# Gate and up of two SwiGLU layers from seven block products in place of eight

## The chip, the cores and the metric

The kernel runs on one core of a Trainium2 chip. Five engines work beside each other there: TensorE (PE in the profile) for matrix products, VectorE (DVE), ScalarE (ACT), GpSimd (POOL) and SyncE (SP), which here issues the loads; 16 transfer engines move the data. What counts is the device time of one execution in microseconds (us), the median over runs.

## What is computed

A trunk of two layers over 512 tokens of width 1024, float32. Each layer has a token mixer (differential attention in layer 0, a gated short convolution in layer 1) and a SwiGLU of hidden width 2816, each followed by a scaled residual and a layer norm. The change touches the SwiGLU:

```
def swiglu(x, w_gate, w_up, w_down):
    h = silu(x @ w_gate) * (x @ w_up)          # x: 512 x 1024, h: 512 x 2816
    return h @ w_down
...
    h = layer_norm(ALPHA * h + mixer(h), ln1_g[i], ln1_b[i])
    h = layer_norm(ALPHA * h + swiglu(h, ...), ln2_g[i], ln2_b[i])
```

## The kernel before

**A product.** TensorE multiplies float32r arrays. `split` (L52) turns a float32 array into two of them: the high part is a cast on ACT (L54), the low part a subtraction on DVE (L55). `mm3` (L70) then multiplies high by high, high by low and low by high, three products per pair of tiles, into one bank of PSUM, of which there are eight.

**Weights.** `weights` (L62) loads 512 KB as 128 x 1024 float32 into one of three `raw` buffers through SP's queue, and splits it into `whi` and `wlo`, six buffers of each. They serve all stages in turn, so that loads and splits run ahead of TensorE until the buffers are full.

**SwiGLU** (`swiglu`, L468). The hidden width is 22 tiles of 128 (`ft`). For one of them `load` fetches two weight tiles, gate and up in each; `part` issues 8 input tiles x 2 x 3 = 48 products with 512 columns, one column per token. `finish` takes silu of gate on ACT (L495), multiplies by up on DVE (L496) and splits the result into `hT`, which the down-projection reads. The first two tiles (`lead`) are done in two halves of 256 tokens, since the tokens of the second half aren't there yet: the normalization of the last two token tiles of the stage before runs meanwhile, and their transposes (`turns`) stand among the lead's products.

**Down-projection** (`project_norm`, L142). It goes over weight tiles of two feature tiles each and over four token tiles, adds the residual, and normalizes (`norm_tile`, L107), with two small operations on POOL for the inverse root. Its `turn` (L127) transposes a normalized token tile on TensorE and splits it into the next stage's input. The same function ends the attention and the convolution.

**Order.** A scheduler places each engine's instructions; each engine goes through its own row in that order, and waits for semaphores of the others. The order at a place can therefore be read from the built program, and its times from the trace.

## Time and profile before

| | us |
|---|---|
| device time, median of 3 runs | 1167.36 |
| lowest and highest of them | 1167.21, 1167.90 |
| span of the profiled execution | 1166.5 |
| TensorE busy in it | 1152.7 |
| DVE, ACT, POOL busy in it | 553.3, 373.3, 62.7 |

The profile is that of one execution. It gives its span, from the first instruction to the last; the device time of that same execution isn't listed apart. The span is 0.9 us below the median. In the rows, L72 is line 72 of the kernel before, a tile's name stands without its buffer number, and a product's tile name says what it serves: `gu` gate and up, `o_wo` and `o_dn` the projections back, `tp_` a transpose. The duration of a product in a row is modelled and overlaps the next one's; the distance from start to start is what counts. For an operation of another engine, the brackets behind it tell how long the engine was idle before it and what ended that. In layer 0 the SwiGLU begins at 252.0 us and its down-projection at 494.4 us; in layer 1 it begins at 795.4 us.

### The profile page before, as it was taken

How to read it: one execution, taken by the hardware profiler on the slowest of the kernel's cores; microseconds unless marked ns; L12 is line 12 of the kernel's file. 1: busy time of each engine (PE TensorE's matmuls, PEld its weight loads, DVE VectorE, ACT ScalarE, POOL GpSimd, SP SyncE). 2: the span in 40 equal slices, each digit the busy share in tenths (PEclk: the TensorE clock that was granted, in tenths of full speed). 3: DMA queues.
4: the chain of work that ended last, by engine and by line, in shares of the span. 5: the costliest groups of instructions: out<-in, count | busy, mean ns of one | idle time of the engine just before them, and what ended most of it. 6: DMA issues, size and time to landing. Idle time of an engine off the chain costs nothing.

```text
span 1166.5 us, 14313 instructions
## 1 busy us (share of the span) xinstructions
PE 1152.7 (99%) x5850; PEld 966.4 (83%) x5850; DVE 553.3 (47%) x861; ACT 373.3 (32%) x634; POOL 62.7 (5%) x83
## 2 busy tenths in 40 slices
PE   9999999999999999999999999999999999999997
PEld 7877787789888888888889888889888888888886
DVE  7777877684333333322355544457433333322316
ACT  5554645423223323311212423313322332321110
POOL 1111112020000000000010000011000000000002
PEclk9999999999999999999999999999999999999999
DMA  8421222134233233233313433323323323333302
GB/s 294 166 73 37 75 70 75 55 95 128 85 108 102 82 106 104 81 105 108 91 55 111 143 95 104 91 72 123 115 87 109 98 84 108 102 98 90 104 23 73
DMA packets 33490, 114.45 MB, mean 98 GB/s; under 512 B 3952, under 2 KB 4848, under 8 KB 33424
## 3 DMA queue, kind: packets, MB, share of 16 engines
q1 hardware_dynamic: 33424, 113.54, 30.8%
q8 instruction: 46, 0.75, 0.3%
q14 instruction: 20, 0.16, 0.0%
HBM read 111.42 MB, written 2.10 MB: 97 GB/s over the span
## 4 chain that ended last, share of the span: by engine, by line
PE 88%; DVE 6%; ACT 3%; POOL 1%; issue 1%; DMA 0%; SPq 0%; POOLq 0%; DVEq 0%; ACTq 0%
PE gu L74 14%; PE gu L72 14%; PE gu L73 14%; PE o_dn L73 7%; PE o_dn L74 7%; PE o_dn L72 7%; PE in L72 4%; PE in L73 4%; PE in L74 4%; ACT p L363 1%; PE o_wco L72 1%; PE o_wco L73 1%; PE o_wco L74 1%; DVE nm L360 1%; PE o_wo L72 1%; PE o_wo L74 1%
## 5 line engine op out<-in xcount | busy, mean ns | idle before, releaser
L72 PE MATMUL gu<-x_hi,whi_gu 128*128 128x512 f32 (+1 forms) x768 | 285.5, 372 | 0.0
L73 PE MATMUL gu<-x_lo,whi_gu 128*128 128x512 f32 (+1 forms) x768 | 285.2, 371 | 0.0
L74 PE MATMUL gu<-x_hi,wlo_gu 128*128 128x512 f32 (+1 forms) x768 | 285.2, 371 | 0.0
L55 DVE TENSOR_TENSOR wlo_gu<-raw_gu,whi_gu 128x1024 fp32r<-128x1024 f32 x88 | 107.7, 1223 | 244.2 <-ACT whi_gu L54 244.2
L73 PEld LDWEIGHTS gu<-x_lo,whi_gu 128*128 128x128 f32 x768 | 144.7, 188 | 25.1
L74 PEld LDWEIGHTS gu<-x_hi,wlo_gu 128*128 128x128 f32 x768 | 144.6, 188 | 25.1
L72 PEld LDWEIGHTS gu<-x_hi,whi_gu 128*128 128x128 f32 x768 | 144.7, 188 | 24.7
L54 ACT CAST whi_gu<-raw_gu 128x1024 fp32r<-128x1024 f32 x88 | 92.7, 1053 | 151.6 <-PE gu L73 130.2
L72 PE MATMUL o_dn<-whi_dn,hT_hi 128*128 128x512 f32 (+1 forms) x352 | 134.9, 383 | 0.0
L73 PE MATMUL o_dn<-wlo_dn,hT_hi 128*128 128x512 f32 (+1 forms) x352 | 134.8, 383 | 0.0
L74 PE MATMUL o_dn<-whi_dn,hT_lo 128*128 128x512 f32 (+1 forms) x352 | 134.6, 382 | 0.0
L55 DVE TENSOR_TENSOR wlo_dn<-raw_dn,whi_dn 128x1024 fp32r<-128x1024 f32 x44 | 53.9, 1224 | 161.9 <-ACT whi_dn L54 161.9
L54 ACT CAST whi_dn<-raw_dn 128x1024 fp32r<-128x1024 f32 x44 | 46.4, 1054 | 161.3 <-PE o_dn L74 117.8
L72 PE MATMUL in<-x_hi,whi_in 128*128 128x512 f32 (+1 forms) x240 | 83.3, 347 | 0.0
L73 PE MATMUL in<-x_lo,whi_in 128*128 128x512 f32 (+1 forms) x240 | 83.2, 347 | 0.0
L74 PE MATMUL in<-x_hi,wlo_in 128*128 128x512 f32 (+1 forms) x240 | 83.2, 347 | 0.0
L495 ACT ACTIVATE sg<-gu 128x512 f32<-128x512 f32 x44 | 26.3, 597 | 170.4 <-PE gu L74 170.4
L72 PEld LDWEIGHTS o_dn<-whi_dn,hT_hi 128*128 128x128 f32 x352 | 66.2, 188 | 13.1
L73 PEld LDWEIGHTS o_dn<-wlo_dn,hT_hi 128*128 128x128 f32 x352 | 66.2, 188 | 13.0
L74 PEld LDWEIGHTS o_dn<-whi_dn,hT_lo 128*128 128x128 f32 x352 | 66.1, 188 | 12.8
L72 PEld LDWEIGHTS in<-x_hi,whi_in 128*128 128x128 f32 x240 | 45.4, 189 | 5.7
L74 PEld LDWEIGHTS in<-x_hi,wlo_in 128*128 128x128 f32 x240 | 45.4, 189 | 5.7
(164 smaller groups left out, 1587.3 us busy)
## 6 DMA issues: line engine op xcount, KB each, us to landing
raw_gu<-in_wgu SPq DMA_DIRECT2D x88, 512.0 KB, 3.6
raw_dn<-in_wdn SPq DMA_DIRECT2D x44, 512.0 KB, 3.6
raw_in<-in_win SPq DMA_DIRECT2D x24, 512.0 KB, 3.5
raw_qk<-in_wqk SPq DMA_DIRECT2D x14, 512.0 KB, 3.6
raw_v<-in_wv SPq DMA_DIRECT2D x8, 512.0 KB, 4.1
raw_wo<-in_wo SPq DMA_DIRECT2D x8, 512.0 KB, 3.6
raw_wco<-in_wco SPq DMA_DIRECT2D x8, 512.0 KB, 3.7
res<-in_xT SPq DMA_DIRECT2D x8, 256.0 KB, 5.6
```

The lines of the kernel that those rows point to most:

```text
L54: nc.scalar.copy(hi, src)
L55: nc.vector.tensor_tensor(lo, src, hi.bitcast(F32), op=ALU.subtract)
L72: nc.tensor.matmul(out, lh, rh, start=first, stop=False)
L73: nc.tensor.matmul(out, lh, rl, start=False, stop=False)
L74: nc.tensor.matmul(out, ll, rh, start=False, stop=last)
L360: nc.vector.tensor_reduce(nm, ps[c][:, :n], axis=AX.X, op=ALU.max, negate=True)
L363: nc.scalar.activation(pc[:, :n], ps[c][:, :n], AF.Exp, bias=nm, accum_out=sm)
L495: nc.scalar.activation(sg, ps[0], AF.Silu)
```

## The change

Gate and up of two hidden tiles form a matrix of 1024 x 512, cut into four blocks: 11 and 21 are gate's upper and lower half of the input features, 12 and 22 are up's. The input is cut likewise: x11 and x12 are the two halves of the features for tokens 0 to 255, x21 and x22 those for tokens 256 to 511. Of the eight products of blocks, Strassen's form (in Winograd's variant) needs seven:

- 11 with x11 and 21 with x12 (their sum is gate of the first tokens, bank `x`)
- t2 with s2, t3 with s3, t4 with x22 (bank `y`), and t1 with s1, 22 with s4 (bank `z`)

where t1 = 12 - 11, t2 = 22 - t1, t3 = 22 - 12, t4 = 21 - t2 for the weights and s1 = x21 + x22, s2 = s1 - x11, s3 = x11 - x21, s4 = x12 - s2 for the input. A layer has 11 such units (`UNITS`). Each product is 24 matrix products with 256 columns (2 hidden tiles x 4 feature tiles x 3). The gate and up of both token halves come out of sums of the three banks, with seven operations on DVE a unit (`u2`, `w5`, `c21`, `h`), a copy `e` of the first product and two silus on ACT. Before the change that was one silu, one cast and two DVE operations per hidden tile.

The four sums of weights are computed on DVE and split as before (`combined`). The blocks 11, 21 and 22 are split in another way (`plain`): ACT writes the high part into `whi`, and minus the raw block, rounded to float32r and so minus the high part, into `wlo`; then a transfer issued by POOL adds the raw block to `wlo`, which leaves the low part. There are 33 of these transfers a layer, 512 KB each, from SBUF to SBUF.

The first three units (`LEAD`) begin with their products of 11 and 21 alone, which need only the first tokens. The two turns that are left over stand behind the first and the second of them; `turn_forms` now also computes the sums s1 to s4 and splits all seven forms of the input. Then these units' other five products follow, for which blocks 11 and 21 are loaded a second time: six loads more a layer, 100 in place of 88 in both. Raw blocks 11 and 22 use the three `raw` buffers, 12 and 21 two new ones (`raw2`).

The hidden `h` stays float32 (11 tiles of 128 x 1024 a layer) until the beginning of the down-projection, where ACT and DVE split it.

The core of the diff:

```diff
+HALF = S // 2
+UNITS = KF // 2
+LEAD = 3
...
+    def turn_forms(tt, r, x, name):
+        ts = slice((tt % 2) * P, (tt % 2 + 1) * P)
+        tps = []
+        for hf in range(2):
+            tp = bank(f"tp_{name}_{tt}_{hf}")
+            for j in range(4):
+                c = hf * 512 + j * P
+                nc.tensor.transpose(tp[:, j * P : (j + 1) * P], r[:, c : c + P], ident)
+            tps.append(tp.rearrange("p (k q) -> p k q", k=4))
+        def form(key, src):
+            hi, lo = x[key]
+            split(hi[:, :, ts], lo[:, :, ts], src)
+        a, b, c, d = (x["raw_" + key][:, :, ts] for key in ("x11", "x12", "x21", "s3"))
+        if tt < 2:
+            form("x11", tps[0])
+            nc.scalar.copy(a, tps[0])
+            form("x12", tps[1])
+            nc.scalar.copy(b, tps[1])
+            return
+        nc.scalar.copy(c, tps[0])
+        nc.vector.tensor_tensor(d, a, tps[0], op=ALU.subtract)
+        nc.vector.tensor_tensor(c, c, tps[1], op=ALU.add)
+        form("s1", c)
+        form("x22", tps[1])
+        nc.vector.tensor_tensor(a, c, a, op=ALU.subtract)
+        form("s2", a)
+        form("s3", d)
+        nc.vector.tensor_tensor(b, b, a, op=ALU.subtract)
+        form("s4", b)
...
-    def swiglu(i, xT, turns, xT_next, out):
+    def swiglu(i, x, turns, open_next, out):
...
-            def load(ft):
-                return [
-                    weights(t["wgu"][i, ft][:, 4 * g : 4 * g + 4, :], 4, 256, f"gu{i}_{ft}_{g}")
-                    for g in range(2)
-                ]
-            def part(ps, wgs, ts, after=()):
-                for n in range(2 * KD):
-                    k, j = (n % 8, n // 8) if ts.stop - ts.start == S else (n // 2, n % 2)
-                    wg, cs = wgs[k // 4], slice(j * P, (j + 1) * P)
-                    mm3(ps[j][:, ts], (wg[0][:, k % 4, cs], wg[1][:, k % 4, cs]),
-                        (xT[0][:, k, ts], xT[1][:, k, ts]), k == 0, k == KD - 1)
-                    for at, f in after:
-                        if at == n:
-                            f()
-            def finish(ft, ps):
-                sg = fwork.tile([P, S], F32, tag="sg", name=f"sg{i}_{ft}")
-                nc.scalar.activation(sg, ps[0], AF.Silu)
-                nc.vector.tensor_tensor(sg, sg, ps[1], op=ALU.mult)
-                split(hT[0][:, ft, :], hT[1][:, ft, :], sg)
-            lead = 2
-            wgs, pss = [], []
-            for ft in range(lead):
-                wgs.append(load(ft))
-                pss.append([bank(f"gu{i}_{ft}_{j}") for j in range(2)])
-            part(pss[0], wgs[0], slice(0, 256), [(8, turns[0])])
-            part(pss[1], wgs[1], slice(0, 256), [(5, turns[1])])
-            for ft in range(lead):
-                part(pss[ft], wgs[ft], slice(256, 512))
-                finish(ft, pss[ft])
-            for ft in range(lead, KF):
-                wg = load(ft)
-                ps = [bank(f"gu{i}_{ft}_{j}") for j in range(2)]
-                part(ps, wg, slice(0, S))
-                finish(ft, ps)
...
+            def blocks(u, keys):
+                out = {}
+                for key in keys:
+                    a, b = int(key[0]) - 1, int(key[1]) - 1
+                    tag, pool, n = ("raw", wpool, 3) if a == b else ("raw2", wk, 2)
+                    raw = pool.tile([P, 4, 256], F32, tag=tag, name=f"raw_gu{i}_{u}_{key}", bufs=n)
+                    nc.sync.dma_start(raw, t["wgu"][i, u, a, b])
+                    out[key] = raw
+                return out
+            def pair(name):
+                hi = wpool.tile([P, 4, 256], F32R, tag="whi", name=f"whi_{name}")
+                lo = wpool.tile([P, 4, 256], F32R, tag="wlo", name=f"wlo_{name}")
+                return hi, lo
+            def plain(raw, name):
+                hi, lo = pair(name)
+                nc.scalar.copy(hi, raw)
+                nc.scalar.activation(lo, raw, AF.Copy, scale=-1.0)
+                nc.gpsimd.dma_start(lo, raw, accum_op=ALU.add)
+                return hi, lo
+            def combined(raw, name):
+                hi, lo = pair(name)
+                split(hi, lo, raw)
+                return hi, lo
+            def tsum(a, b, op, name):
+                r = wk.tile([P, 4, 256], F32, tag="t", name=name, bufs=3)
+                nc.vector.tensor_tensor(r, a, b, op=op)
+                return r
+            def product(ps, w, key, first):
+                xh, xl = x[key]
+                for f in range(2):
+                    o = ps[:, f * HALF : (f + 1) * HALF]
+                    fs = slice(f * P, (f + 1) * P)
+                    for k in range(4):
+                        wh, wl = w[0][:, k, fs], w[1][:, k, fs]
+                        for n, (a, b) in enumerate(((wh, xh), (wh, xl), (wl, xh))):
+                            nc.tensor.matmul(o, a, b[:, k, :], start=first and f + k + n == 0,
+                                             stop=k == 3 and n == 2, skip_group_check=True)
...
+            def start(u, raw):
+                s = {"x": bank(f"x{i}_{u}")}
+                product(s["x"], plain(raw["11"], f"gu{i}_{u}_11"), "x11", True)
+                if u < LEAD:
+                    both = slot(slots["xa"], f"h{UNITS - 5 - u}", (2, 512), F32, f"lead{i}_{u}")
+                    s["e"], s["g"] = both[:, 0, :], both[:, 1, :]
+                else:
+                    s["e"], s["g"] = temp("e", u, 2), temp("g", u)
+                nc.scalar.copy(s["e"], s["x"])
+                return s
+            def second(u, s, raw):
+                product(s["x"], plain(raw["21"], f"gu{i}_{u}_21"), "x12", False)
+                nc.scalar.activation(s["g"], s["x"], AF.Silu)
+            def rest(u, s, raw, whole):
+                nm = f"gu{i}_{u}_"
+                v = nc.vector.tensor_tensor
+                t1 = tsum(raw["12"], raw["11"], ALU.subtract, nm + "t1")
+                t2 = tsum(raw["22"], t1, ALU.subtract, nm + "t2")
+                y = bank(f"y{i}_{u}")
+                product(y, combined(t2, nm + "t2"), "s2", True)
+                u2 = temp("u2", u)
+                v(u2, s["e"], y, op=ALU.add)
+                z = bank(f"z{i}_{u}")
+                product(z, combined(t1, nm + "t1"), "s1", True)
+                w5 = temp("w5", u)
+                v(w5, s["e"], z, op=ALU.add)
+                if whole:
+                    second(u, s, raw)
+                t3 = tsum(raw["22"], raw["12"], ALU.subtract, nm + "t3")
+                product(y, combined(t3, nm + "t3"), "s3", False)
+                v(w5, w5, y, op=ALU.add)
+                t4 = tsum(raw["21"], t2, ALU.subtract, nm + "t4")
+                product(z, plain(raw["22"], nm + "22"), "s4", False)
+                h = hidden(u)
+                hid[u] = h
+                v(u2, u2, z, op=ALU.add)
+                v(h[:, :, :HALF], s["g"].rearrange("p (f q) -> p f q", f=2),
+                  u2.rearrange("p (f q) -> p f q", f=2), op=ALU.mult)
+                product(y, combined(t4, nm + "t4"), "x22", False)
+                c21 = temp("c21", u)
+                v(c21, s["e"], y, op=ALU.add)
+                nc.scalar.activation(c21, c21, AF.Silu)
+                v(h[:, :, HALF:], c21.rearrange("p (f q) -> p f q", f=2),
+                  w5.rearrange("p (f q) -> p f q", f=2), op=ALU.mult)
+            state = {}
+            for u in range(LEAD):
+                state[u] = start(u, blocks(u, ("11",)))
+                if u < 2:
+                    turns[u]()
+            for u in range(LEAD):
+                second(u, state[u], blocks(u, ("21",)))
+            for u in range(UNITS):
+                if u < LEAD:
+                    rest(u, state[u], blocks(u, ("11", "12", "22", "21")), False)
+                else:
+                    raw = blocks(u, ("11", "12", "22", "21"))
+                    rest(u, start(u, raw), raw, True)
...
+            hT = []
+            for u in range(UNITS):
+                if u == 0:
+                    hi = wpool.tile([P, 2, S], F32R, tag="whi", name=f"hid{i}_{u}_hi")
+                    lo = wpool.tile([P, 2, S], F32R, tag="wlo", name=f"hid{i}_{u}_lo")
+                elif u < 8:
+                    hi, lo = (slot(slots["f"], f"f{2 * u - 2 + j}", (2, S), F32R, f"hid{i}_{u}_{j}") for j in range(2))
+                else:
+                    hi, lo = (slot(dx, f"d{2 * u + j}", (2, S), F32R, f"hid{i}_{u}_{j}") for j in range(2))
+                split(hi, lo, hid[u])
+                hT.append((hi, lo))
...
-    gu = np.stack([a["ffn_w_gate"].reshape(2, KD, P, KF, P), a["ffn_w_up"].reshape(2, KD, P, KF, P)], axis=4)
+    gu = np.stack([a[f"ffn_w_{n}"].reshape(2, 2, 4, P, UNITS, 256) for n in ("gate", "up")], axis=2)
```

**Where the order of work changes.** First ACT's row in the lead of layer 0, behind the last high part of the first blocks. Names: `lead0_0` is the copy of bank x of unit 0, `gu0_1_21` block 21 of unit 1, `x1_s3` a form of the input; L564 and L565 are the two ACT operations of `plain`, L57 a cast of `split`. Before:

```order
L54 CAST whi_gu0_2_0_3135<-raw_gu0_2_0_3133 128x1024
L54 CAST x1_hi_2353<-tp_wo_2_0_2930 128x4x128
L54 CAST x1_hi_2353<-tp_wo_2_1_2937 128x4x128
L54 CAST whi_gu0_2_1_3141<-raw_gu0_2_1_3139 128x1024
L54 CAST x1_hi_2353<-tp_wo_3_0_2983 128x4x128
L54 CAST x1_hi_2353<-tp_wo_3_1_2990 128x4x128
L54 CAST whi_gu0_3_0_3202<-raw_gu0_3_0_3200 128x1024
L495 ACT_TABLE_LOAD
L495 ACTIVATE sg0_0_3075<-gu0_0_0_2887 128x512
```

After:

```order
L608 COPY lead0_0_2933<-x0_0_2903 128x512
L189 COPY x1_raw_x21_2680<-tp_wo_2_0_2935 128x4x128
L564 CAST whi_gu0_0_21_3055<-raw_gu0_0_21_3053 128x1024
L57 CAST x1_s3_hi_2674<-x1_raw_s3_2681 128x4x128
L565 ACTIVATE wlo_gu0_0_21_3056<-raw_gu0_0_21_3053 128x1024
L57 CAST x1_s1_hi_2668<-x1_raw_x21_2680 128x4x128
L57 CAST x1_x22_hi_2670<-tp_wo_2_1_2940 128x4x128
L57 CAST x1_s2_hi_2672<-x1_raw_x11_2678 128x4x128
L57 CAST x1_s4_hi_2676<-x1_raw_x12_2679 128x4x128
L608 COPY lead0_1_2992<-x0_1_2962 128x512
L189 COPY x1_raw_x21_2680<-tp_wo_3_0_2994 128x4x128
L564 CAST whi_gu0_1_21_3087<-raw_gu0_1_21_3085 128x1024
```

Between the two operations on block 21 of unit 0 and those of unit 1 there are now the copies of the banks, which wait for TensorE, and the turns' casts; the second operation on block 21 of unit 1 (`L565 ACTIVATE wlo_gu0_1_21`) comes six rows further down.

Second, SP's row of loads at the same place; `raw_gu0_0_21` is block 21 of unit 0. Before:

```order
L64 DMA raw_gu0_2_0_3133<-in_wgu 128x1024
L64 DMA raw_gu0_2_1_3139<-in_wgu 128x1024
L64 DMA raw_gu0_3_0_3200<-in_wgu 128x1024
L64 DMA raw_gu0_3_1_3206<-in_wgu 128x1024
L102 DMA g_f0_4473<-in_ln2_g 128x1024
L103 DMA b_f0_4474<-in_ln2_b 128x1024
L64 DMA raw_gu0_4_0_3267<-in_wgu 128x1024
L64 DMA raw_gu0_4_1_3273<-in_wgu 128x1024
```

After:

```order
L552 DMA raw_gu0_0_21_3053<-in_wgu 128x1024
L552 DMA raw_gu0_1_21_3085<-in_wgu 128x1024
L114 DMA g_f0_5589<-in_ln2_g 128x1024
L115 DMA b_f0_5590<-in_ln2_b 128x1024
L552 DMA raw_gu0_2_21_3117<-in_wgu 128x1024
L552 DMA raw_gu0_0_12_3151<-in_wgu 128x1024
L552 DMA raw_gu0_0_21_3155<-in_wgu 128x1024
```

A load waits for its buffer. With two buffers for blocks 12 and 21, the load of 21 of unit 2 waits for the adding transfer of unit 0's block 21, the load of 12 of unit 0 for that of unit 1's, and the second load of 21 of unit 0 for that of unit 2's. All rows behind them on SP wait as well.

Third, DVE's row between two units in the middle of layer 0, where `gu0_9_t3` is a sum of weights and `wlo_gu0_9_t2` a low part. Before:

```order
L55 TENSOR_TENSOR wlo_gu0_10_0_3672<-raw_gu0_10_0_3669,whi_gu0_10_0_3671 128x1024
L496 TENSOR_TENSOR sg0_7_3530<-sg0_7_3530,gu0_7_1_3481 128x512
L55 TENSOR_TENSOR wlo_gu0_10_1_3678<-raw_gu0_10_1_3675,whi_gu0_10_1_3677 128x1024
L55 TENSOR_TENSOR hT_lo0_2874<-sg0_7_3530,hT_hi0_2873 128x512
L55 TENSOR_TENSOR wlo_gu0_11_0_3739<-raw_gu0_11_0_3736,whi_gu0_11_0_3738 128x1024
L496 TENSOR_TENSOR sg0_8_3597<-sg0_8_3597,gu0_8_1_3548 128x512
```

After:

```order
L58 TENSOR_TENSOR wlo_gu0_8_t4_5035<-gu0_8_t4_5000,whi_gu0_8_t4_5034 128x1024
L576 TENSOR_TENSOR gu0_9_t3_5203<-raw_gu0_9_22_5070,raw_gu0_9_12_5068 128x1024
L623 TENSOR_TENSOR u20_8_4906<-e0_8_4870,y0_8_4877 128x512
L627 TENSOR_TENSOR w50_8_4937<-e0_8_4870,z0_8_4908 128x512
L58 TENSOR_TENSOR wlo_gu0_9_t2_5113<-gu0_9_t2_5109,whi_gu0_9_t2_5112 128x1024
L58 TENSOR_TENSOR wlo_gu0_9_t1_5144<-gu0_9_t1_5107,whi_gu0_9_t1_5143 128x1024
L576 TENSOR_TENSOR gu0_9_t4_5234<-raw_gu0_9_21_5072,gu0_9_t2_5109 128x1024
L632 TENSOR_TENSOR w50_8_4937<-w50_8_4937,y0_8_4877 128x512
L576 TENSOR_TENSOR gu0_10_t1_5341<-raw_gu0_10_12_5302,raw_gu0_10_11_5300 128x1024
L637 TENSOR_TENSOR u20_8_4906<-u20_8_4906,z0_8_4908 128x512
L638 TENSOR_TENSOR h0_8_5031<-g0_8_4871,u20_8_4906 128x2x256
L58 TENSOR_TENSOR wlo_gu0_9_t3_5206<-gu0_9_t3_5203,whi_gu0_9_t3_5205 128x1024
```

For each hidden tile there were two low parts of weights, one product with up and one low part of the hidden. For each unit of two tiles there are now four sums, four low parts and seven operations on the banks; the weights are a unit ahead of the banks that they stand among.

## Rows read from the trace of the kernel before

**Rows 1.** The page: busy us, share, count by engine; granted clock in 40 slices.

```profile
PE 1152.7 (99%) x5850; PEld 966.4 (83%) x5850; DVE 553.3 (47%) x861; ACT 373.3 (32%) x634; POOL 62.7 (5%) x83
...
PEclk9999999999999999999999999999999999999999
```

**Rows 2.** Stretches: sum, then busy us of PE, PEld, DVE, ACT, POOL; PEclk, DMA.

```profile
252.00:276.00 24.00, 24.00 (x203) 23.99 (x202) 15.28 (x21) 8.51 (x11) 1.70 (x2) 1.00 0.48 155
276.00:494.00 218.00, 218.00 (x967) 180.64 (x966) 75.46 (x81) 64.96 (x81) 0.00 (x0) 1.00 0.31 99
```

**Rows 3.** Groups by shape: count, busy us, mean ns, idle us before.

```profile
L72 PE MATMUL gu<-x_hi,whi_gu 128*128 128x512 f32 x640 | 249.0, 389 | 0.0
...
L72 PE MATMUL gu<-x_hi,whi_gu 128*128 128x256 f32 x128 | 36.5, 285 | 0.0
...
L72 PEld LDWEIGHTS gu<-x_hi,whi_gu 128*128 128x128 f32 x768 | 144.7, 188 | 24.7
```

**Rows 4.** TensorE in time order, wide products: start us, duration us, instruction.

```profile
420.26 0.39 PE L72 MATMUL gu<-x_hi,whi_gu 128*128 128x512 f32 x1
...
435.90 0.39 PE L72 MATMUL gu<-x_hi,whi_gu 128*128 128x512 f32 x1
```

**Rows 5.** The same, narrow products of layer 0's lead.

```profile
252.00 0.28 PE L72 MATMUL gu<-x_hi,whi_gu 128*128 128x256 f32 x1
...
262.00 0.28 PE L72 MATMUL gu<-x_hi,whi_gu 128*128 128x256 f32 x1
...
271.71 0.28 PE L72 MATMUL gu<-x_hi,whi_gu 128*128 128x256 f32 x1
```

**Rows 6.** Tile o_dn (down-projections): ns min/median/max, first and last start.

```profile
L72 PE MATMUL o_dn<-whi_dn,hT_hi x352: 277/389/476, 494.4 to 1155.4; 128*128 128x512 f32 x172, 128*128 128x256 f32 x4
```

**Rows 7.** Groups of ACT and DVE, columns as in rows 3.

```profile
L54 ACT CAST whi_gu<-raw_gu 128x1024 fp32r<-128x1024 f32 x88 | 92.7, 1053 | 151.6 <-PE gu L73 130.2 <-PE o_wco L74 9.3 <-PE o_wo L74 7.5
...
L54 ACT CAST hT_hi<-sg 128x512 fp32r<-128x512 f32 x44 | 27.0, 613 | 0.0
...
L55 DVE TENSOR_TENSOR wlo_gu<-raw_gu,whi_gu 128x1024 fp32r<-128x1024 f32 x88 | 107.7, 1223 | 244.2 <-ACT whi_gu L54 244.2
...
L496 DVE TENSOR_TENSOR sg<-sg,gu 128x512 f32<-128x512 f32 x44 | 30.2, 687 | 30.1 <-PE gu L74 25.4 <-ACT sg L495 4.7
...
L55 DVE TENSOR_TENSOR wlo_wo<-raw_wo,whi_wo 128x1024 fp32r<-128x1024 f32 x8 | 11.2, 1402 | 3.3 <-ACT whi_wo L54 3.2
```

**Rows 8.** Transfers: packets, MB, engine share; issues: KB each, us to landing.

```profile
q1 hardware_dynamic: 33424, 113.54, 30.8%
...
raw_gu<-in_wgu SPq DMA_DIRECT2D x88, 512.0 KB, 3.6
...
res<-in_x SPq DMA_DIRECT2D x1, 2048.0 KB, 9.9
```

**Rows 9.** A group of POOL, columns as in rows 3.

```profile
L90 POOL TENSOR_TENSOR rstd_wo<-ve_wo,mhalf 128x1 f32<-128x1 f32 x4 | 3.7, 929 | 0.3
```

**Rows 10.** ACT in time order, layer 0's lead; brackets: idle us, releaser.

```profile
255.87 1.08 ACT L54 CAST x_hi<-tp_wo 128x512 fp32r<-128x512 f32 x2 [3.97 <-PE tp_wo L132]
...
261.41 1.08 ACT L54 CAST x_hi<-tp_wo 128x512 fp32r<-128x512 f32 x2 [3.44 <-PE tp_wo L132]
...
270.88 1.28 ACT L495 ACT_TABLE_LOAD   x1 [1.64 <-PE gu L74]
```

**Rows 11.** The same of ACT and POOL, end of the attention.

```profile
221.30 1.05 ACT L54 CAST whi_gu<-raw_gu 128x1024 fp32r<-128x1024 f32 x1 [0.81 <-PE o_wo L74]
...
222.95 0.70 POOL L405 TENSOR_SCALAR ms<-ms 128x2 f32<-128x2 f32 x1 [5.95 <-ACT on L403]
```

**Rows 12.** TensorE in time order at the start of the kernel.

```profile
7.38 0.63 PE L72 MATMUL k<-x_hi,whi_qk 128*128 128x512 f32 x1 [1.25 <-ACT whi_qk L54]
...
10.37 0.63 PE L74 MATMUL q<-x_hi,wlo_qk 128*128 128x512 f32 x1
```

**Rows 13.** That stretch, columns as in rows 2.

```profile
9.00:12.00 3.00, 3.00 (x10) 2.34 (x9) 2.75 (x5) 2.51 (x5) 0.00 (x0) 0.67 1.03 379
```

93 lines of the change are left out of this document (66 added, 27 removed).

## Prediction

> **What bounds the kernel now.** The page's busy shares come first: TensorE is busy for 1152.7 of 1166.5 us, DVE for under half, and the granted clock is at its upper level in every slice [rows 1]. Then the windows by stage: in the stretch with half-width products and in the one with full-width ones TensorE has no gap, while DVE works for 75 and ACT for 65 of 218 us [rows 2]. So the SwiGLU stages last as long as their products are issued, and the change is worth what it saves there, less whatever now makes TensorE wait. The third view is the pace. Between the two rows of a 512-column product lie 69 steps from one product to the next, 15.64 us / 69 = 0.2267 us [rows 4]; between the last two of a 256-column one 81, 9.71 / 81 = 0.120 us [rows 5]. By columns alone the second would be 0.113, so about 13 ns of each product don't shrink with it. The counts check it: 640 x 3 wide and 128 x 3 narrow products in two layers [rows 3] give 960 x 0.2267 + 192 x 0.120 = 240.7 us a layer; first product to first down-projection is 252.0 to 494.4, 242.4 us with 1.7 us of transposes [rows 5, 6].
>
> **Products.** 11 units x 7 blocks x 24 products of 256 columns = 1848 a layer: 1848 x 0.120 = 221.8 us, 18.9 less, **37.8 for both layers.** As many columns in wide products would take 924 x 0.2267 = 209.5 and save 31 a layer; the narrow form gives the rest back.
>
> The Trainium skill, "TensorE: Matmul & The Clock Gate", section Back-to-back issue gap, gives for an isolated product N/2.4 + 2.5 ns: 109 and 216 ns. By it the saving would be an estimated 26 us a layer and the time some 15 us lower; the spacing of 120 ns read here decides against it.
>
> **The new way to a weight's low part.** Blocks 11, 21 and 22 get it from ACT (high part, then minus raw: 2 x 1.05 us [rows 7]) and an accumulating transfer that POOL issues, 33 a layer. The trace has no such transfer. Call X the time from POOL's turn to its landing. Lower bound: an ordinary 512 KB load, 3.6 us. Upper bound: the 2 MB load, 9.9 us, plus a POOL instruction of 0.9, 10.8 [rows 8, 9]. I take the one that reads as moving twice the bytes, 1 MB: 3.6 + (9.9 - 3.6) / 3 = 5.7, plus 0.9 = **6.6 us**, since an add must fetch both the raw block and what it adds to.
>
> The skill's "Collectives: The Full Stack", section Stop 4 (why a reduce-scatter is half of an all-gather), says that an add in the transfer path reads two sources and so runs at half a copy's rate. No run here shows it yet. With a copy's price my sum below would be 1143, with the doubled one 1149.
>
> **Steady state, units 3 to 10 (20.2 us each).** ACT: ten casts of 1.05 and three of 0.6 = 12.3 us. DVE: four combinations and four low parts at 1.22, seven operations on 512 columns at 0.69 = 14.6 us [rows 7]. Both fit under TensorE. There are six pairs of weight buffers and seven blocks a unit, so a block's pair comes free five products (14.4 us) before it is needed; less ACT's 2.1, an accumulate has 12.3 us. At X of 6.6 or even 10.8 that hides it. Cost nothing, cover 5.7 us. The hidden split of the down-projection (11 x 1.05 on ACT, 1.22 on DVE) goes beside groups of 24 products, 5.4 us each: 2.1 of ACT and 2.4 of DVE in each, nothing. In units 0 to 2 the rest has five products, 14.4 us, against DVE's 14.6, with the restarts about 1 us a layer: **+2**.
>
> **The lead of layer 0.** Here the pipeline is empty, and ACT's rows decide (the order shown ahead). Times from 252.0, the first narrow product [rows 5]: x_0 until 254.9, turn, x_1 until 258.6, turn, x_2 until 262.4. The next product, 21 of unit 0, wants its low part. ACT's minus raw of it stands behind the copy of x_0, the first turn's copy, its high part and a cast: done at 259.6, landed at 266.2, **3.8 us of waiting**. In before, ACT at that place did one turn's casts (1.08) and waited 3.97 and 3.44 us for TensorE [rows 10]. Unit 1: ACT's minus raw stands behind e_1, a copy, hi, e_2 (x_2 ends at 262.4) and four casts: 268.1, landed 274.8, while TensorE is free at 269.1: **5.7**. Unit 2: behind it are the table load (1.28 [rows 10]), a silu and a cast; 272.7, landed 279.3, TensorE free at 277.7: **1.6**. The first combined block: SP's load of 12 waits in raw2's two buffers for the landing at 274.8, then 3.6 for the load, two combinations, hi and lo, 283.1 against 282.2: **0.9**. Sum 12.0. With X = 3.6 it is 9.0, with X = 10.8 it is 18.7.
>
> A long wait has a second price. Before TensorE starts in earnest it waits 1.25 us and works thinly; from 7.38 to 10.37 the wide products then come every 0.427 us, near twice 0.2267, and the granted clock of that stretch is 0.67, between its levels of 1.2 and 2.4 GHz: eight products, 1.6 us lost [rows 12, 13]. I charge this to the two longest waits: **+3.2** (bounds 0 and, with five waits, 8).
>
> In layer 1 ACT's rows put both first minus raws ahead of the copy of x_0; the same walk gives **+1.5** (0 at X = 3.6, 10 at 10.8). At the end of the attention one more ACT operation of 1.05 stands ahead of the last head's squares, and its accumulate ahead of POOL's ms, on which the transpose waits [rows 11]: **+1**.
>
> **Sum.** -37.8 + 12.0 + 3.2 + 1.5 + 1 + 2 = -18.1. The profiled span of 1166.5 becomes 1148.4; the median of before, 1167.36, is 0.9 more than that span, so **1149 us**. With X = 3.6 it is 1143 (9.0 in the lead, one fall of the clock, nothing in layer 1), with 10.8 it is 1169 (18.7, five falls, 10).
>
> **Rivals.**
> 1. *The accumulates bind the 16 transfer engines: slower.* Ordinary transfers took 30.8% of 1166.5 us for 113.54 MB, 3.16 us a MB, 1.66 for 512 KB [rows 8]. A unit of 20.2 us needs four loads, 6.6, and three accumulates. At 1 MB's price (3.3) that is 16.6, 82%, no bound; it binds above 4.5 us an accumulate, and from about 4.9 (a gain of 18.1 us lost over 16 units, 1.1 each of which a third falls on one accumulate) the kernel is slower than before. If it costs what 2 MB does, 6.6, a unit is 26.5 and the time 1149 + 16 x 6.3 = **1250**. For: nothing in before shows the rate of an accumulate, and 6.6 of 20.2 us are taken ahead of it. Against: it needs nearly three times a copy's price. Chance 0.14.
> 2. *Only the latency is long* (X 8 to 11): the waits of both leads grow, **1157 to 1171**; from X = 10 the gain is gone. Chance 0.13.
> 3. *DVE becomes the bound.* In the attention stage, where POOL works too, DVE's low parts took 1402 instead of 1223 ns [rows 7]; at 15% more on all its operations a unit takes 16.7 of 20.2, and only the five-product units suffer, 2.3 each: +12, **1162**. It would need 38% to bind everywhere. Chance 0.04.
> 4. *The narrow pace doesn't hold.* A weight load lasts 188 ns [rows 3]; were the narrow products spaced by it, a layer would last 1848 x 0.188 = 347 us, and the time be some **1380**. The break-even is 240.7 / 1848 = 0.130 us. Against it: in the lead of before the weight loads fill 23.99 of 24.00 us and the spacing is still 0.120 [rows 2, 5]. Chance 0.02. In a sentence by itself: the section named above also lists sustained spacings of 81 ns at 128 and 131 ns at 512 columns, by which half-width products would hardly be cheaper and this change would lose an estimated 36 us a layer; the 0.2267 here contradicts it.
> 5. *The waits of the lead are shorter than walked* (the queue's casts run earlier, no fall of the clock): the time is **1132 to 1143**, the end without any loss being 1130 (1167.4 - 37.8). Chance 0.12.
> 6. *The change doesn't do what it says.* It does remove an eighth of the columns: 1848 x 256 against 960 x 512 + 192 x 256, 0.875. What else it says, that the hidden stays float32, costs nothing above.
>
> **How the numbers follow.** The forecast case (X of 4 to 8, waits of 9 to 16 us) has 0.55 and reaches from 1143 to 1157. The range adds the latency case and the upper two thirds of case 5: 1136 to 1172 holds 0.55 + 0.13 + 0.08 + 0.04 = 0.80; left out are case 1 (0.14), case 4 and the rest of 5. A measurement of this kernel tells 0.2%, 2.3 us, from no change. Faster by more: 0.55 + 0.12 + 0.04 + 0.07 (half of case 2) = 0.78. Within: 0.04. Slower: 0.14 + 0.02 + 0.02 = 0.18.
>
> **What would show it.** The narrow products should be 0.120 us apart in the units of 20.2 us, and TensorE's idle time lie in some 40 us behind the end of each mixer, in waits for transfers issued by POOL. The median from POOL's issue to landing is X. Wrong: a unit longer than 20.5 us with TensorE waiting for a transfer (case 1) or for DVE (case 3), a granted clock below 1 outside the leads, or a spacing other than 0.120.

## The result

| | before | after |
|---|---|---|
| device time, median, us | 1167.63 | 1150.47 (1142.02 to 1151.14, 4 executions) |
| ratio to before, 95% interval | | 0.983 (0.980 to 0.986) |
| span of the profiled execution, us | 1166.5 | 1148.3 |

The forecast was 1149 us. The page of after, against [rows 1] and [rows 8]; the last two lines are issues with KB each and median us from issue to landing:

```profile
PE 1119.0 (97%) x7242; PEld 999.1 (87%) x7242; DVE 737.4 (64%) x1065; ACT 520.8 (45%) x790; POOL 119.6 (10%) x149
...
PEclk9999999998999999999999999999899999999998
...
q1 hardware_dynamic: 35152, 119.83, 33.8%
q0 software_dynamic: 9504, 34.61, 16.5%
...
raw_gu<-in_wgu SPq DMA_DIRECT2D x100, 512.0 KB, 4.6
wlo_gu<-raw_gu POOLq DMA_DIRECT2D x66, 512.0 KB, 5.8
```

TensorE now has some 3% of idle time, and the granted clock is below its upper level in three slices: the 10th and the 29th are the two leads, the last is the kernel's end. A new queue, q0, carries the adding transfers; the kernel moves 155.6 MB in place of 114.5. The first products and first down-projection products in the two traces cut the span into five stages:

| stage | before, us | after, us | change | forecast |
|---|---|---|---|---|
| to the first narrow product | 252.0 | 250.1 | -1.9 | +1 |
| gate and up of layer 0 | 242.4 | 234.3 | -8.1 | -2.7 |
| down-projection, convolution | 301.0 | 305.0 | +4.0 | 0 |
| gate and up of layer 1 | 242.4 | 228.3 | -14.1 | -16.4 |
| last down-projection, end | 128.7 | 130.6 | +1.9 | 0 |
| sum | 1166.5 | 1148.3 | -18.2 | -18.1 |

So the total was met by stages that were each off by 2 to 5 us. Three things make up the differences: what the leads wait for, how far apart the products are, and the start-up. TensorE's wait there was 1.25 us in [rows 12] and 0.4 in this execution, and the granted clock of the stretch of [rows 13] was 0.67 there and 1.00 here. Of the 1.9 us of the first stage 1.3 are there at 20 us, where both kernels still do the same work. In the traces of the experiments below, most of which change nothing in this stage, it lasts from 250.2 to 253.4 us.

**The lead of layer 0.** TensorE's rows in order of time (start us, us, in brackets the idle time before):

```profile
260.44 0.28 PE L588 MATMUL x<-x_x_lo,whi_gu 128*128 128x256 f32 x1
265.74 0.58 PE L588 MATMUL x<-x_x_hi,wlo_gu 128*128 128x256 f32 x1 [5.02 <-DMA wlo_gu<-raw_gu]
266.12 0.41 PE L588 MATMUL x<-x_x_hi,whi_gu 128*128 128x256 f32 x1
266.33 0.41 PE L588 MATMUL x<-x_x_lo,whi_gu 128*128 128x256 f32 x1
...
272.94 0.39 PE L588 MATMUL x<-x_x_hi,whi_gu 128*128 128x256 f32 x1 [1.71 <-ACT whi_gu L564]
...
278.69 0.58 PE L588 MATMUL x<-x_x_hi,wlo_gu 128*128 128x256 f32 x1 [2.66 <-DMA wlo_gu<-raw_gu]
...
292.35 0.38 PE L588 MATMUL z<-x_s_hi,wlo_gu 128*128 128x256 f32 x1 [0.56 <-DMA wlo_gu<-raw_gu]
```

The first wait is that of block 21 of unit 0 for its low part. Behind it the products come 0.21 us apart, not 0.12: the clock has fallen, as the stretch from 266 to 270 us shows (columns as in [rows 2]), which [rows 13] had shown at the kernel's start:

```profile
266.00:270.00 4.00, 4.00 (x20) 4.00 (x21) 1.69 (x3) 2.33 (x3) 0.85 (x1) 0.50 0.78 195
```

The second wait, of 1.7 us, is put down to ACT; counted from 265.74, the product that waited is the third of unit 1 (its record is missing), the first one to read a low part that POOL issued at 267.35. Where the first wait comes from stands in the chain that ended last (start us, us, what):

```profile
247.42 4.63 DMA wlo_gu<-raw_gu
252.48 4.58 DMA raw_gu<-in_wgu
259.92 5.78 DMA wlo_gu<-raw_gu
265.75 3.50 DMA raw_gu<-in_wgu
```

POOL's and ACT's rows of the same stretch:

```profile
247.42 0.94 POOL L566 DMA_DIRECT2D wlo_gu<-raw_gu  x1
...
257.08 1.05 ACT L564 CAST whi_gu<-raw_gu 128x1024 fp32r<-128x1024 f32 x1 [2.90 <-DMA raw_gu<-in_wgu]
...
258.56 1.06 ACT L565 ACTIVATE wlo_gu<-raw_gu 128x1024 fp32r<-128x1024 f32 x1
```

At 247.42 POOL issues the addition for block 11 of unit 2. Its landing frees the raw buffer for which SP's row waits with the second load of block 11 of unit 1; the load of block 21 of unit 0, which TensorE needs first, stands behind that one and lands at 257.1. Then follow ACT's two operations and the next addition, at 259.92, and for its landing SP waits with the load of block 21 of unit 2, at 265.75: the third wait. All of layer 0's waits come to 10.0 us, those of layer 1 (2.2, 1.9, 0.2 and 1.3) to 5.6.

**The units behind the leads** have no wait: the stretch 340 to 400 of after, to be held against the second of [rows 2], shows TensorE busy throughout, DVE at 71%, ACT at 59% and the transfer engines at 76% where they were at 31%.

```profile
340.00:400.00 60.00, 60.00 (x512) 60.00 (x511) 42.52 (x46) 35.12 (x40) 7.74 (x9) 1.00 0.76 173
```

**The spacing.** Spacing is the distance from the start of one product to that of the next. Narrow products in the middle of layer 0, 102 steps, 0.1178 us each (0.120 in [rows 5]); then wide ones in its down-projection, 42 steps of 0.2333 us, and a little later 39 steps of 0.2267, the spacing of [rows 4]:

```profile
349.81 0.28 PE L588 MATMUL y<-x_s_hi,whi_gu_t 128*128 128x256 f32 x1
...
361.82 0.28 PE L588 MATMUL z<-x_s_hi,whi_gu 128*128 128x256 f32 x1
...
506.00 0.39 PE L75 MATMUL o_dn<-whi_dn,hid 128*128 128x512 f32 x1
...
515.80 0.39 PE L75 MATMUL o_dn<-whi_dn,hid 128*128 128x512 f32 x1
...
533.88 0.39 PE L75 MATMUL o_dn<-whi_dn,hid 128*128 128x512 f32 x1
...
542.72 0.39 PE L75 MATMUL o_dn<-whi_dn,hid 128*128 128x512 f32 x1
```

The same line issues them, with the same shapes. What differs is the tile `hid`: for units 1 to 7 it lies in the pool of the input's forms, allocated at the other end of SBUF (`side="right"`), for units 8 to 10 in a pool at the usual end.

### The profile page after: what moved, and what is told of

It reads as the page before. It is cut to its first block, busy times and chain, and to the rows that moved or that the text cites. A ratio compares the mean times of both kernels' runs of the same rounds, so it can differ in the third digit from the quotient of the medians.

```text
span 1148.3 us, 17876 instructions
## 1 busy us (share of the span) xinstructions
PE 1119.0 (97%) x7242; PEld 999.1 (87%) x7242; DVE 737.4 (64%) x1065; ACT 520.8 (45%) x790; POOL 119.6 (10%) x149
## 3 DMA queue, kind: packets, MB, share of 16 engines
q0 software_dynamic: 9504, 34.61, 16.5%
## 4 chain that ended last, share of the span: by engine, by line
PE 81%; DVE 6%; issue 4%; ACT 3%; DMA 3%; POOL 1%; SPq 0%; POOLq 0%; DVEq 0%; ACTq 0%
PE y L588 15%; PE z L588 10%; PE x L588 9%; PE o_dn L77 7%; PE o_dn L76 7%; PE o_dn L75 7%; PE in L75 4%; PE in L77 4%; PE in L76 4%; DMA wlo_gu<-raw_gu 2%; ACT p L426 1%; PE o_wco L75 1%; PE o_wco L77 1%; PE o_wco L76 1%; DVE nm L423 1%
## 5 line engine op out<-in xcount | busy, mean ns | idle before, releaser
L58 DVE TENSOR_TENSOR wlo_gu_t<-gu_t,whi_gu_t 128x1024 fp32r<-128x1024 f32 x88 | 106.9, 1221 | 30.4 <-ACT whi_gu_t L57 30.2
L57 ACT CAST whi_gu_t<-gu_t 128x1024 fp32r<-128x1024 f32 x88 | 90.9, 1047 | 75.3 <-DVE gu_t L576 29.6
L75 PE MATMUL o_dn<-whi_dn,hid 128*128 128x512 f32 (+1 forms) x320 | 123.8, 387 | 0.0
L77 PE MATMUL o_dn<-whi_dn,hid 128*128 128x512 f32 (+1 forms) x320 | 123.8, 387 | 0.0
L76 PE MATMUL o_dn<-wlo_dn,hid 128*128 128x512 f32 (+1 forms) x320 | 123.8, 387 | 0.0
L588 PE MATMUL x<-x_x_hi,wlo_gu 128*128 128x256 f32 x352 | 101.5, 288 | 9.6 <-DMA wlo_gu<-raw_gu 9.6
L57 ACT CAST whi_dn<-raw_dn 128x1024 fp32r<-128x1024 f32 x44 | 46.1, 1052 | 141.0 <-PE o_dn L77 107.5
L588 PE MATMUL x<-x_x_hi,whi_gu 128*128 128x256 f32 x352 | 101.7, 289 | 3.9 <-ACT lead L608 2.2
L566 POOL DMA_DIRECT2D wlo_gu<-raw_gu x66 | 57.5, 871 | 436.6 <-ACT wlo_gu L565 324.1
L588 PE MATMUL x<-x_x_lo,whi_gu 128*128 128x256 f32 x352 | 101.1, 287 | 0.0
L588 PE MATMUL y<-x_s_hi,wlo_gu_t 128*128 128x256 f32 x352 | 98.3, 279 | 0.2 <-DVE wlo_gu_t L58 0.2
L588 PE MATMUL y<-x_s_lo,whi_gu_t 128*128 128x256 f32 x352 | 98.4, 280 | 0.0
L588 PE MATMUL y<-x_s_hi,whi_gu_t 128*128 128x256 f32 x352 | 98.4, 279 | 0.0
L564 ACT CAST whi_gu<-raw_gu 128x1024 fp32r<-128x1024 f32 x66 | 69.2, 1050 | 62.7 <-PE y L588 28.4
L565 ACT ACTIVATE wlo_gu<-raw_gu 128x1024 fp32r<-128x1024 f32 x66 | 69.7, 1056 | 12.0 <-PE o_wco L76 8.7
```

Source lines behind the costliest of these rows:

```text
L57: nc.scalar.copy(hi, src)
L58: nc.vector.tensor_tensor(lo, src, hi.bitcast(F32), op=ALU.subtract)
L75: nc.tensor.matmul(out, lh, rh, start=first, stop=False)
L76: nc.tensor.matmul(out, lh, rl, start=False, stop=False)
L77: nc.tensor.matmul(out, ll, rh, start=False, stop=last)
L564: nc.scalar.copy(hi, raw)
```

## Experiments

Each kernel was timed beside the kernel before on the same chip, whose medians were 1167.2 to 1167.5 us. A ratio is to those.

### The changed kernel again, and its lead mended in two ways

The theory: what is lost against the bare products lies in the leads, and is the adding transfer's time to landing, ACT's order, SP's late load and the fall of the clock. The rival: the adding transfers cost time all along.

**The changed kernel again.**

> The changed kernel once more, beside the kernel before on the same chip. Theory A (the times of its stages belong to the program): about 1150 us, waits of 5.0, 1.7 and 2.7 us of TensorE in the lead of layer 0, 2.2, 1.9 and 1.3 in that of layer 1, wide products of the down-projections 0.2317 us apart (0.2267 in the kernel before) and narrow ones 0.1178 (0.1200). Theory B (the two spacings belong to the execution or its chip): the same waits, but the spacings of the kernel before, and then some 1142 us, the lowest of the four times on record.

1149.05 us (ratio 0.984, 0.983 to 0.986). All spacings were those of the first trace (0.1178, and 0.231 on average in a down-projection). The waits differ by up to 1.5 us: in layer 0 they were 4.4, 1.9, 1.4 and 2.1 us in place of 5.0, 1.7, 2.7 and 0.6. Theory A: the spacings belong to the program, and not to an execution or a chip. That left open what in the program sets them.

**Block 21 of the lead in the other buffers.**

```
-            def blocks(u, keys):
+            def blocks(u, keys, early=False):
...
-                    tag, pool, n = ("raw", wpool, 3) if a == b else ("raw2", wk, 2)
+                    tag, pool, n = ("raw", wpool, 3) if a == b or early else ("raw2", wk, 2)
...
-                second(u, state[u], blocks(u, ("21",)))
+                second(u, state[u], blocks(u, ("21",), True))
```

> The lead's loads of block 21 take the three buffers of blocks 11 and 22 in place of the two others, which puts them ahead of all second loads on SP and lets ACT and POOL do their splits before the copies of bank x. Theory A (the lost time is the lead's: a late load, ACT's order, the adding transfer's 5.8 us, and the clock that falls behind the waits): layer 0's lead loses under 3 us in place of 14, layer 1's under 3 in place of 8, so 1131 to 1139 us. Rival (the adding transfers cost time all along the units): 1146 to 1150 us.

1136.72 us (0.974, 0.973 to 0.976). TensorE's rows with a wait, layer 0:

```profile
265.63 0.39 PE L588 MATMUL x<-x_x_hi,wlo_gu 128*128 128x256 f32 x1 [1.08 <-DMA wlo_gu<-raw_gu]
...
269.86 0.39 PE L588 MATMUL x<-x_x_hi,wlo_gu 128*128 128x256 f32 x1 [1.13 <-DMA wlo_gu<-raw_gu]
...
274.24 0.38 PE L588 MATMUL y<-x_s_hi,whi_gu_t 128*128 128x256 f32 x1 [1.52 <-ACT whi_gu_t L57]
...
275.50 0.39 PE L588 MATMUL y<-x_s_hi,wlo_gu_t 128*128 128x256 f32 x1 [0.76 <-DVE wlo_gu_t L58]
```

The wait of 5.0 us is gone and the others are near 1. The clock still falls: behind the last two of them, from 276.5 to 279.5 us, the products come 0.213 us apart.

```profile
276.40:279.70 3.30, 3.30 (x18) 3.30 (x16) 2.74 (x3) 2.53 (x4) 0.86 (x1) 0.50 0.25 88
```

Gate and up of layer 0 take 227.0 us in place of 234.3. So the place of the load in SP's row, which the prediction did not walk, was needed for the longest wait; the next kernel shows that the addition was needed too. The time lies in theory A's range, but neither layer got there as expected. The bare products and transposes take 219.4 us a layer (1848 x 0.1178 and 1.7). Layer 0 loses 7.5 us against that, not under 3. Layer 1 still waits 4.6 us for the first combined block, and its 220.4 us (228.3 in after) come from a spacing of 0.1133 us from 818 us on, of which more below. At 0.1178 they would be 227.7, and the profiled execution, 1135.8, some 1143 (an estimate), between the two ranges.

**Low parts by DVE in the lead alone.**

```
-                product(s["x"], plain(raw["11"], f"gu{i}_{u}_11"), "x11", True)
+                product(s["x"], (combined if u < LEAD else plain)(raw["11"], f"gu{i}_{u}_11"), "x11", True)
...
-                product(s["x"], plain(raw["21"], f"gu{i}_{u}_21"), "x12", False)
+                product(s["x"], (combined if u < LEAD else plain)(raw["21"], f"gu{i}_{u}_21"), "x12", False)
```

> In the first three units alone the low parts of blocks 11 and 21 are made by DVE's subtraction, as before the change, in place of ACT's second operation and the adding transfer; SP's order stays nearly as it is. Theory A: the adding transfer's 5.8 us disappear from each of the lead's waits; the first load of block 21 still lands at 257 us, so waits of 0 to 2 us, no fall of the clock, 1132 to 1139 us. Rival (SP's late load alone makes the waits): 1144 to 1150 us.

1144.8 us (0.979, 0.977 to 0.982): the number of the rival, but not its reason. The chain of the additions is gone, and with it the wait of 5.0 us; in its place TensorE waits for DVE, which forms the input's sums at that time, and for ACT:

```profile
265.72 0.39 PE L588 MATMUL x<-x_x_hi,wlo_gu 128*128 128x256 f32 x1 [0.30 <-DVE wlo_gu L58]
...
270.81 0.58 PE L588 MATMUL x<-x_x_hi,wlo_gu 128*128 128x256 f32 x1 [2.23 <-DVE wlo_gu L58]
...
276.74 0.39 PE L588 MATMUL y<-x_s_hi,whi_gu_t 128*128 128x256 f32 x1 [1.62 <-ACT whi_gu_t L57]
```

So neither theory had it right: without the addition the leads are some 4 us shorter (1144.8 against 1149.05), and what comes next behind it is DVE, which I had not put on the lead's path.

**Low parts by DVE everywhere.**

```
             def plain(raw, name):
                 hi, lo = pair(name)
-                nc.scalar.copy(hi, raw)
-                nc.scalar.activation(lo, raw, AF.Copy, scale=-1.0)
-                nc.gpsimd.dma_start(lo, raw, accum_op=ALU.add)
+                split(hi, lo, raw)
```

> All low parts are made by DVE; no adding transfer is left. DVE then has 11 operations of 1.22 and seven of 0.69 us in a unit of seven products: 18.2 of 19.8 us (narrow products 0.1178 apart). Theory A (the adding transfer costs nothing behind the lead): within 4 us of the kernel with DVE in the lead alone, 1132 to 1141 us, and slower only where the first units have five products. Rival 1 (the transfers take time from the steady units): more than 4 us faster than that kernel. Rival 2 (DVE becomes the bound at 92%): 1150 us or more, with TensorE waiting for DVE in every unit.

1143.92 us (0.979, 0.978 to 0.981), 0.9 less than with DVE in the lead alone. The same stretch as above:

```profile
340.00:400.00 60.00, 60.00 (x512) 60.00 (x511) 55.41 (x60) 27.01 (x31) 0.00 (x0) 1.00 0.37 115
```

DVE is busy for 92%, the transfer engines for 37% in place of 76%, and TensorE has no gap in either. Behind the leads the adding transfers neither cost nor give anything that shows here; DVE would just have carried the whole split. That is the prediction's "cost nothing" for units 3 to 10, seen from the other side.

### What the transfer engines bear

**Every adding transfer twice.**

```
                 nc.gpsimd.dma_start(lo, raw, accum_op=ALU.add)
+                nc.gpsimd.dma_start(lo, raw, accum_op=ALU.add)
```

> Every adding transfer is issued twice, so that the low parts of blocks 11, 21 and 22 are not what they should be and the output is not the reference's; all else is the changed kernel. The adding queue's 16.5% of 1148.3 us for 66 transfers are 2.9 us of all engines each, an ordinary load 1.7: a unit of 19.8 us needs 6.8 + 3 x 2.9 = 15.4 us of them now and 24.1 then. Theory A (the engines are the limit, and lie not far away): 4.3 us more in each of 16 units, and the waits of the leads up by some 25 us: 1220 to 1245 us. Rival (only the time to landing counts, and 11.6 us still hide behind six pairs of buffers): the leads alone, 1165 to 1180 us.

1269.05 us (1.087, 1.084 to 1.089), nearest to theory A, but above its range. TensorE's waits (us in all, times, longest), and the same stretch:

```profile
PE x L589 <- DMA wlo_gu<-raw_gu: 48.1, 16, 9.8
PE z L589 <- DMA wlo_gu<-raw_gu: 42.6, 16, 4.9
```

```profile
340.00:400.00 60.00, 50.86 (x415) 49.91 (x414) 32.38 (x36) 26.70 (x30) 13.94 (x16) 0.97 0.92 213
```

415 products in 60 us are 24.3 us for a unit's 168, where 24.1 had been worked out from 1.7 us for a load and 2.9 for an addition. The engines are 92% busy. The waits also bring the clock down (0.97 in the stretch), which the range had left out. But the number alone doesn't show that the engines are the limit, for POOL's row gives it as well. The second addition into a block (L567) waits on POOL for the landing of the first, 61 times and 376.0 us in all, and the next block's first addition (L566) stands behind it:

```profile
348.10 0.86 POOL L567 DMA_DIRECT2D wlo_gu<-raw_gu  x1 [6.45 <-DMA wlo_gu<-raw_gu]
348.75 1.13 POOL L566 DMA_DIRECT2D wlo_gu<-raw_gu  x1
356.39 0.87 POOL L567 DMA_DIRECT2D wlo_gu<-raw_gu  x1 [6.52 <-DMA wlo_gu<-raw_gu]
356.97 1.18 POOL L566 DMA_DIRECT2D wlo_gu<-raw_gu  x1
```

From 356.97 to 523.97 us POOL's row takes 8.35 us a block, 25.0 for a unit's three, and from 370.1 to 520.2 TensorE takes 25.0 us a unit. The median from issue to landing is 6.3 us, little above the 5.8 of after. So in this kernel POOL's row, one landing at a time, is enough to explain the time, and whether the engines alone would bind is not shown. Rival 1 of the prediction stays an estimate: by these shares it would bind at 19.8 us = 6.8 + 3a, a = 4.3 us for an addition if the engines could be busy throughout, and the kernel runs at 2.9.

### What narrow products cost

**The kernel before, all gate and up products on 256 columns.**

```
-                part(ps, wg, slice(0, S))
+                part(ps, wg, slice(0, 256))
+                part(ps, wg, slice(256, 512))
                 finish(ft, ps)
```

> The kernel before the change, with all its gate and up products on 256 columns, as in its first two hidden tiles: 1920 products of 512 columns become 3840 of 256. Theory A (the narrow spacing is the program's, 0.1200 us in this form): 1920 x (0.2400 - 0.2267) = 25.5 us more, 1193 us. Theory B (the narrow spacing can also be the 0.1178 of the changed kernel): 17 us more, 1184 us. Rival (no price for narrow products at all): 1168 us.

1195.1 us (1.023, 1.021 to 1.026), theory A with its 0.1200 us. Gate and up of a layer take 255.2 us in place of 242.4, so halving the width costs 25.5 us in both; 1.4 us of the rest lie ahead of the first narrow product (253.4 in place of 252.0). It also shows that 0.1200 belongs to the kernel before, and 0.1178 to something that the change brought along.

### Why the spacing changed

**Smaller tiles for the split hidden, at the same end of SBUF.**

```
-            hT = (
-                ffn.tile([P, KF, S], F32R, name=f"hT_hi{i}"),
-                ffn.tile([P, KF, S], F32R, name=f"hT_lo{i}"),
-            )
+            hT = [
+                tuple(ffn.tile([P, 2, S], F32R, name=f"hT_{j}{i}_{c}") for j in ("hi", "lo"))
+                for c in range(KF // 2)
+            ]
...
```

> The kernel before the change, with its split hidden in one tile for each pair of feature tiles, high and low part in turn, as the changed kernel has it, in place of two large tiles; the instructions are the same. Theory A (the wider spacing of the down-projection, 0.2317 for 0.2267 us, comes from where the stationary operand lies within its pool): the down-projections go to about 0.2317 and the time to 1171 to 1174 us. Rival (it comes from something else in the changed program): 0.2267 and 1167 us.

1167.7 us (1.000, 0.999 to 1.001), spacing 0.2267: the rival. Tile sizes and the order of high and low parts in a pool make no difference here.

**The split hidden at the other end.**

```
-            ffn = fctx.enter_context(tc.tile_pool(name=f"ffn{i}", bufs=1))
+            ffn = fctx.enter_context(tc.tile_pool(name=f"ffn{i}", bufs=1, side="right"))
```

> The kernel before the change; only the pool of the split hidden lies at the other end of SBUF, where the changed kernel keeps the forms of the input, seven eighths of the split hidden and zT. All engines' rows are the same. Theory A (the spacing of the wide products depends on which end of SBUF the stationary operand lies at: in the changed kernel's down-projections the feature tiles at this end come 0.2333 us apart, those at the other end 0.2267): 0.2333 in both down-projections, 1056 x 0.0066 = 7 us more, 1174 us. Rival (it belongs to the changed program in another way): 0.2267 and 1167 us.

1173.68 us (1.006, 1.004 to 1.007). 42 steps of 0.2333 us in the down-projection, between these two rows:

```profile
505.78 0.40 PE L72 MATMUL o_dn<-whi_dn,hT_hi 128*128 128x512 f32 x1
...
515.58 0.40 PE L72 MATMUL o_dn<-whi_dn,hT_hi 128*128 128x512 f32 x1
```

**The transposed input at the other end.**

```
+    xpool = ctx.enter_context(tc.tile_pool(name="xpool", bufs=1, side="right"))
...
-        hi = act.tile([P, KD, S], F32R, tag="xT_hi", name=f"{name}_hi")
-        lo = act.tile([P, KD, S], F32R, tag="xT_lo", name=f"{name}_lo")
+        hi = xpool.tile([P, KD, S], F32R, tag="xT_hi", name=f"{name}_hi")
+        lo = xpool.tile([P, KD, S], F32R, tag="xT_lo", name=f"{name}_lo")
```

> The kernel before the change; only the pool of the transposed input, the moving operand of gate and up and of the convolution's input projection, lies at the other end of SBUF. Theory A (for a moving operand the same end makes wide products 0.2289 in place of 0.2267 us apart and narrow ones 0.1178 in place of 0.1200): gate and up lose 1920 x 0.0022 = 4.2 us and win 384 x 0.0022 = 0.8, the projections of attention and convolution a little of each: 1169 to 1172 us. Rival (the narrow 0.1178 is the Strassen form's own): 0.1200 and 0.2267 as before, 1167 us.

1170.72 us (1.003, 1.002 to 1.004). Wide gate and up products come 0.2289 us apart (63 steps between the two rows), those of the lead 0.1178, and the down-projections keep 0.2267:

```profile
300.18 0.39 PE L75 MATMUL gu<-x_hi,wlo_gu 128*128 128x512 f32 x1
...
314.60 0.39 PE L75 MATMUL gu<-x_hi,wlo_gu 128*128 128x512 f32 x1
```

That is theory A in both experiments, with the size that it gave. The weights stay where they were; moving the other operand's pool to the right end of SBUF is enough. There a stationary operand adds 6.6 ns to a wide product, a moving one adds 2.2 to a wide and takes 2.2 from a narrow one. Why that is so, and whether it is the end or the address that counts, no run shows. (The changed kernel has 7 of 11 pairs of the split hidden at that end, not the seven eighths that the first of the two expectations says.)

### The two mends together, and a spacing that switches

**Block 21 in the three buffers, its low part by DVE in the lead.** The edits are those of the kernels of 1136.7 and 1144.8 us, the latter for block 21 alone.

> The lead's loads of block 21 in the three buffers, as in the kernel of 1136.7 us, and their low parts by DVE; blocks 11 stay with the adding transfer. There TensorE still waited 4.6 us in one layer and less in the other for the first combined block, whose load of block 22 stood behind an adding transfer. Theory A: that wait shrinks by 2 to 5 us in each layer, 1127 to 1134 us. Rival (DVE, which forms the input at that time, becomes the one that is late): 1135 to 1141 us.

1139.3 us (0.976, 0.974 to 0.978), the five executions at 1132.84 and 1139.1 to 1140.7. By its median it is the rival's: the wait for the first combined block is 2.4 and 3.0 us (1.5 and 4.6 in the kernel of 1136.7 us), and DVE works without a gap through that stretch of layer 0. The execution of 1132.84 is the profiled one. In its layer 1 something else happens (TensorE in order of time):

```profile
815.08 0.28 PE L588 MATMUL z<-x_s_hi,whi_gu 128*128 128x256 f32 x1
815.20 0.28 PE L588 MATMUL z<-x_s_lo,whi_gu 128*128 128x256 f32 x1
815.63 0.39 PE L588 MATMUL z<-x_s_hi,wlo_gu 128*128 128x256 f32 x1 [0.16 <-DMA wlo_gu<-raw_gu]
...
829.79 0.28 PE L588 MATMUL z<-x_s_hi,whi_gu 128*128 128x256 f32 x1
...
841.69 0.28 PE L588 MATMUL y<-x_s_hi,whi_gu_t 128*128 128x256 f32 x1
```

After a wait of 0.16 us for the low part of block 22 the products are 0.1133 us apart (105 steps between the last two rows), and stay so to the end of the layer. In the kernel of 1136.7 us the same happened at 818.6 us, behind a wait of under 0.1 us for the same block. Its time thus holds a switch, and theory A's range was set from it. At 0.1178 in both layers it would take the 1143 us estimated above, and this kernel takes 1139.4 (the next run): at one spacing the two mends together are some 3 to 4 us better than the first alone.

**The same kernel once more.**

> The kernel with block 21 in the three buffers and DVE's low parts in the lead once more. Its executions took 1132.8 and 1139 to 1141 us; the profiled one was that of 1132.8, and in it the narrow products of layer 1 came 0.1133 us apart from 815 us on, in place of 0.1178. Theory A (the two times are two spacings, entered by chance at a short wait): an execution of about 1139.5 us shows 0.1178 in all of both layers, one of 1133 shows 0.1133 behind a short wait for block 22's low part, one of 1125 in both layers. Rival (the two times are waits of another length): the spacing of layer 1 is 0.1133 again, at 1139 us.

1139.42 us, with 0.1178 in both layers; no wait for block 22 stands in its layer 1. The same stretch, 102 steps:

```profile
829.93 0.28 PE L588 MATMUL z<-x_s_hi,whi_gu 128*128 128x256 f32 x1
...
841.95 0.28 PE L588 MATMUL y<-x_s_hi,whi_gu_t 128*128 128x256 f32 x1
```

Theory A: the two times are two spacings. Gate and up of layer 1 took 218.5 us with the switch and 226.1 without, and the longest wait in it was 3.0 us both times. Not every short wait switches: the one of 0.56 us in after, shown above, did not. Nor is a short wait needed. In the kernel with every addition twice, the products behind a wait of 2.87 us were 0.1133 us apart (118 steps from 370.12 to 383.49), until further waits, behind which they were 0.1178 again:

```profile
369.90 0.38 PE L589 MATMUL x<-x_x_hi,wlo_gu 128*128 128x256 f32 x1 [2.87 <-DMA wlo_gu<-raw_gu]
370.12 0.28 PE L589 MATMUL x<-x_x_hi,whi_gu 128*128 128x256 f32 x1
...
383.49 0.28 PE L589 MATMUL z<-x_s_lo,whi_gu 128*128 128x256 f32 x1
```

So a restart behind a wait can enter either spacing, and where no further wait comes it stays. That after's fastest execution, 1142.02, is one with a layer at 0.1133 fits its distance (1848 x 0.0045 = 8.3 us), but it left no trace, so this is only argued. What in the wait does it is open.

## Why the prediction was right, step by step

- **Products:** right in kind, mis-sized. 1848 x 0.1178 = 217.7 us, 23.0 less than 240.7 a layer, 46 for both in place of 37.8. The term that failed is the narrow spacing, taken over from the kernel before as a property of the width; 2.2 ns of it hang on the place of the input. The prediction had itself named a spacing other than 0.120 as a sign of being wrong.
- **X:** taken as 6.6 us, measured as 5.8 from POOL's issue to landing, 6.1 with the 0.3 us from ACT's end. An addition takes 16.5% of 1148.3 us / 66 = 2.9 us of all engines against 1.7 for a load of the same size, 1.7 times as much. The doubled price by which I chose between the bounds, and the rule of the Trainium skill ("Collectives: The Full Stack", section "The bandwidth ceiling: the fold count and why AG ≠ RS ≠ AR": the reduce step of a ring needs two source reads and runs at half the rate of a copy), are near it, a little high.
- **Steady state at no cost:** right, by the stretch without a wait and by the kernel without additions, equal to 0.9 us. The +2 for the units with five products is not to be seen: from the last wait of each lead, at 292 and 826 us, to the end of the stage every product comes at 0.1178. No run tests rival 1 by itself.
- **The lead of layer 0:** 12.0 us of waits forecast, 10.0 measured, but split otherwise: 5.0, 1.7, 2.7 and 0.6 in place of 3.8, 5.7, 1.6 and 0.9, and the last of them for block 22, not for the first combined block. The step that failed is the first: I took ACT's row as what decides when block 21 is ready, and left out what SP's row puts ahead of its load. The second wait was shorter because the first was longer and the clock lower.
- **Fall of the clock:** 3.2 forecast. 24 products behind the first wait and 16 behind the third came 0.095 us late each, 3.8 us.
- **Layer 1:** +2.5 forecast, 8.9 measured against the bare 219.4 us (217.7 and the transposes): waits of 5.6, about 1.9 for the clock, the rest in the first steps behind the waits (for the wait of 2.21 us, 2.49 us from start to start, where a step is 0.12). The walk through its better ACT order missed that the copy of unit 2's bank x stands there behind another late load of block 21 (2.2 us), and the additions for block 22.
- **Down-projection and convolution, forecast 0:** +5.9. The work was indeed hidden, but 7 of 11 pairs of the hidden lie at the other end: 2 x 528 x 7/11 x 0.0066 = 4.4 (an estimate that takes all as wide), the convolution's output projection 192 x 0.0066 = 1.3, its input projection 432 x 0.0022 less 288 x 0.0022, 0.3: 6.0.
- **End of the attention, forecast +1:** not to be seen; the stage was 1.9 us shorter, of which 1.3 are the start-up, its wait and its clock, and no part of the change.

By stages the forecast was off by -2.9, -5.4, +4.0, +2.3 and +1.9, in all -0.1. The spacing alone gave 8.1 us that were not foreseen and took 6.0. The mechanism of the forecast, products saved less waits in the leads, holds; that the sum came within 1.5 us is luck: more saved per product, more lost in layer 1 and to the wider spacing, and a start-up that happened to be short.
